# Bringing a softmax's reciprocals to a row: diagonal matrices on TensorE, or a trip through scratch memory

## The chip, the cores and the metric

The kernel runs on one core of a Trainium2 chip. The core has five engines that run side by side and meet at semaphores: TensorE (PE, matrix products into PSUM; its weight loads are shown apart as PEld), VectorE (DVE), ScalarE (ACT), GpSimd (POOL), and SyncE (SP), which here only issues DMAs. Each engine has a queue of its own, in the order in which the program holds its instructions. The metric is the device time of one execution in microseconds (us); lower is better.

## The reference

One layer of an encoder with four token mixers side by side (a long convolution "hyena", a state space "S5", differential attention and latent attention), an output projection, a gated feed-forward net and an embedding gate, for 2048 tokens of width 1024. What matters here are the two attentions, each with 4 heads and values of width 64:

```
# differential attention, per head
attn = softmax(s1) - lam * softmax(s2)      # s1, s2: scores with an ALiBi bias
o    = attn @ v
# latent attention, per head
a    = softmax(s);  o = a @ v
```

Every softmax divides a row of exponentials, a query's, by its sum.

## The kernel before, in words

The kernel is written against a scheduler: the program lists work in an order with priorities, and the scheduler sorts each engine's instructions by its own estimate of when each can start. Two kinds of work are interleaved in the stage that matters. One is attention; the other is a background queue of the other mixers (filters, S5, embedding, the hyena convolution, output weights), advanced a little after every step of attention.

`Attention.run` (line 394) walks 64 units: 4 heads times 16 blocks of 128 queries. A unit handles one head of each attention at once, since both share the stage's shape. Its steps are 12 calls of `chunk`, and beside each the pieces of the unit one or two before it, by a table `PLAN`:

- `chunk` and `scores` (lines 421 and 438): TensorE makes scores of 128 queries by 512 keys in a PSUM bank (line 448), VectorE moves them to SBUF and takes minima (lines 451, 453), and when a row of 2048 is whole, ScalarE exponentiates it in place and sums it (line 458). The sum of a query lies on that query's partition, as `total`, 128 x 1.
- `combine` (line 460) joins the two score rows of the differential attention, on VectorE and, for some heads, GpSimd (lines 465 to 475).
- `scale(hd)` (line 477), once for each of the two attentions: VectorE takes the reciprocal of the sums (line 481), GpSimd multiplies the identity by it, which gives a 128 x 128 diagonal matrix `diag` (line 483).
- `transpose` (line 486): TensorE turns the exponentials so that keys lie on partitions (line 492), ScalarE copies them out of PSUM (line 497).
- `weigh(piece)` (line 499), 8 pieces, two units late: TensorE multiplies the values with them into a PSUM tile `ps_o`, whose partitions are the 64 channels of one head and the 64 of the other, and whose columns are the 128 queries (line 509, shown as L502 in the profile, where the helper is). The result has the queries along a row, whereas the reciprocals lie down a column. So after the last piece, a 128 x 64 matrix of ones is multiplied with each `diag` (line 519, again L502), which puts the 128 reciprocals in a row on all 64 partitions of that head, in the second half of the same PSUM tile. ScalarE copies that row to SBUF (line 523), VectorE multiplies (line 524), and every second unit ScalarE's queue issues two DMAs that write the result to `mixT` in scratch memory (line 527).

`ps_o` has one buffer. Query tiles `q_sb` have two, so a unit's five query loads (lines 381 to 383), on SyncE's queue, wait until the unit two before has made its last scores. The same queue carries the background's loads and stores: in the stretch of the hyena convolution these are `h_f`, `h_g` and `h_sp` (lines 1233 to 1237), each with two buffers. At a head's end it carries ten loads of the next head's keys `k_sb` (lines 369 to 372), which wait for the last scores that read the old ones.

Of the kernel before, what the change touches and what calls it, by code (L numbers as in the profile page):

```python
# [11 lines left out]
F32 = mybir.dt.float32  # L12
# [3 lines left out]
AF = mybir.ActivationFunctionType  # L16
ALU = mybir.AluOpType
PSUM = bass.MemoryType.PSUM

SEQ = 2048  # L20
DM = 1024
# [319 lines left out]
class Attention:  # L341
# [6 lines left out]
    def __init__(self, ops, const, S, ctx):  # L348
        self.ops, self.tc, self.nc, self.S, self.ident = ops, ops.tc, ops.nc, S, const["ident"]
        self.strip, self.neg_lam = const["strip"], const["neg_lam"]  # L350
        pool = lambda name, bufs, **k: ctx.enter_context(ops.tc.tile_pool(name=name, bufs=bufs, **k))
        self.qp, self.kp, self.sp, self.atp = pool("at_q", 2), pool("at_k", 1), pool("at_s", 1), pool("at_t", AT_BUFS[0])
        self.sm, self.op, self.dp, self.vp = pool("at_sm", 4), pool("at_o", 2), pool("at_d", 4), pool("at_v", 1)
        self.ps_s = pool("at_pss", PSS[0], space=PSUM)
        self.ps_t = pool("at_pst", PSS[1], space=PSUM)
        self.ps_o = pool("at_pso", 1, space=PSUM)
        self.ones = self.vp.tile([128, 64], F32, name="at_ones")
        self.nc.vector.memset(self.ones, 1.0)
        self.k, self.v, self.evac = [None] * 4, [None] * 2, 0

    def keys(self, i, h):
# [51 lines left out]
class Unit:  # L413
# [63 lines left out]
    def scale(self, hd):  # L477

        at, nc = self.at, self.nc
        r = at.sm.tile([128, 1], F32, name="r1")  # L480
        nc.vector.reciprocal(r, self.total["s" if hd else "s1"])
        d = at.dp.tile([128, 128], F32, name="diag")
        nc.gpsimd.tensor_scalar(d, at.ident, r, 0.0, ALU.mult, ALU.add)
        self.scales[hd] = d

    def transpose(self, hd, g):
        at, nc = self.at, self.nc
# [11 lines left out]
    def weigh(self, piece):  # L499
# [2 lines left out]
        mm = lambda out, lhsT, rhs, first, last: nc.tensor.matmul(  # L502
            out, lhsT=lhsT, rhs=rhs, start=first, stop=last, skip_group_check=True)
        if piece == 0:
            self.ps = at.ps_o.tile([128, 2, 128], F32, name="ps_o")
        ps = self.ps
        for c in (2 * piece, 2 * piece + 1):
            for hd in range(2):
                inst = mm(ps[ts(hd, 64), 0], at.v[c // 8][:, c % 8, ts(hd, 64)], self.tiles[hd, c // 4][:, c % 4], c == 0,
                          c == 15)  # L510
                if c == hd == 0:

                    for k in range(2):
                        at.ops.after(inst, self.turned[k, 3])
        if piece % 4 == 3 and self.t == 15:
            at.values(piece // 4, self.h + 1)
        if piece == 7:
            for hd in range(2):
                mm(ps[ts(hd, 64), 1], at.ones, self.scales[hd], False, True)
            if self.t % 2 == 0:  # L520
                at.out = at.op.tile([128, 2, 128], F32, name="o_sb")
            o = at.out[:, self.t % 2]
            nc.scalar.activation(o, ps[:, 1], AF.Copy)
            nc.vector.tensor_mul(o, ps[:, 0], o)
            if self.t % 2:
                for hd in range(2):
                    nc.scalar.dma_start(at.S["mixT"][ds(256 * hd + 64 * self.h, 64), ds(128 * self.t - 128, 256)],
# [158 lines left out]
NH = 22  # L686
# [1027 lines left out]
def tile_hybrid_encoder(ctx, tc, A, out):  # L1714
# [2 lines left out]
    pool = lambda c, name, bufs, **k: c.enter_context(tc.tile_pool(name=name, bufs=bufs, **k))  # L1717
    S = {}
    for name, shape in (("zhyT", [768, SEQ]), ("zs5", [SEQ, 256]), ("c", [SEQ, 352]), ("vda", [SEQ, 256]),
                        ("vml", [SEQ, 256]), ("yhs", [SEQ, 512]), ("mixT", [512, SEQ]), ("h", [SEQ, DM]), ("fT", [8, 128, SEQ]), ("f2T", [8, 128, SEQ]), ("g", [NH, 128, SEQ]), ("emb", [SEQ, DM]),  # L1720
                        ("h2", [SEQ, DM]), ("hspec", [2, 2, 2, 16, 128, 128]), ("hyc", [6, 32, 128, 64]), ("hyq", [2, 64, 128, 64]), ("s5_win", [128, 16, 2, 2, 128]),
                        ("s5_wout", [128, 2, 16, 256]), ("s5_g", [16, 16, 496]), ("s5_m", [128, 2, 16, 256]), ("s5_a16", [128, 2, 2, 16])):
        S[name] = tc.dram_tile(shape, F32, name="d_" + name)
# [165 lines left out]
```

## Time and profile before

| | before |
|---|---|
| times of three runs | 3736.25, 3740.24, 3745.21 us |
| median | 3740.24 us |
| profiled execution: time / span in the trace | 3744.99 / 3743.2 us |
[...]
| TensorE, VectorE, ScalarE, GpSimd busy | 91%, 66%, 47%, 41% |
| units of attention | from 585 us to 1905 us of the span |

The profile is one execution. Busy time is the union of an engine's instructions; a wait is an idle stretch of an engine, put down to the instruction elsewhere that ended it. A DMA's issue stands on the queue that issued it, and its landing is counted from there. In the timeline, instructions of one line that follow each other are merged into one row with a count.

### The profile page before, as it was taken

What the parts mean: (1) busy time and instruction counts of PE and PEld (TensorE: products, weight loads), DVE (VectorE), ACT (ScalarE), POOL (GpSimd) and SP (SyncE); (2) the same over time, 40 slices, a digit from 0 to 9 for tenths busy, and PEclk for the clock granted to TensorE, in tenths of its full rate; (3) what the DMA queues carried; (4) which work ended last, traced back from release to release, by engine and by line L of the source; (5) the groups of instructions that cost most, each with busy time, mean ns of one, the idle gap of its engine ahead of it and who ended that gap; (6) DMA issues with size and microseconds to landing.
All of it is one profiled execution on the core that took longest, in us unless ns stands there. A gap on an engine that the chain in (4) does not pass through costs nothing. (4 is left out here: it accounts for less than half of the span.)

```text
span 3743.2 us, 56824 instructions
## 1 busy us (share of the span) xinstructions
PE 3423.1 (91%) x20582; PEld 2802.2 (75%) x20582; DVE 2455.0 (66%) x5109; ACT 1754.3 (47%) x2889; POOL 1553.0 (41%) x1423
## 2 busy tenths in 40 slices
PE   8999997887999899989999899999999987989787
PEld 6889875676778778767777678887888865867666
DVE  6667548974746455677667764447545578688877
ACT  5334316665667545577754443334333433333443
POOL 1324001681852022253355554445544544344554
PEclk9999997998999999999999899999999999999899
DMA  4544655327232795961054532223222254546554
GB/s 143 185 142 153 219 164 141 104 76 208 76 100 87 190 251 146 222 195 40 18 178 144 177 113 79 90 79 107 90 79 90 74 188 149 203 141 191 186 170 151
DMA packets 426698, 518.46 MB, mean 139 GB/s; under 512 B 117003, under 2 KB 319631, under 8 KB 422415
## 3 DMA queue, kind: packets, MB, share of 16 engines
q1 hardware_dynamic: 352368, 407.05, 36.8%
q10 hardware_dynamic: 74048, 107.76, 8.2%
q8 instruction: 163, 2.67, 0.3%
q14 instruction: 119, 0.97, 0.1%
HBM read 340.89 MB, written 178.01 MB: 139 GB/s over the span
## 5 line engine op out<-in xcount | busy, mean ns | idle before, releaser
L448 PE MATMUL ps_s<-k_sb,q_sb 96*128 96x512 f32 x1280 | 437.5, 444 | 53.8 <-DVE at_s L451 22.2
L823 PE MATMUL ps_st<-t_hi,s_hi 128*128 128x512 f32 x984 | 397.2, 404 | 51.8 <-DVE st_sum L850 21.2
L458 ACT ACTIVATE at_s<-at_s,least_s 128x2048 f32<-128x2048 f32 x192 | 384.2, 2003 | 88.3 <-DVE least_s L457 71.6
L453 DVE CUSTOM_DVE_ANT_0 at_s<-ps_s,strip 128x512 f32<-128x512 f32 x512 | 338.1, 685 | 111.2 <-PE ps_s L448 96.9
L823 PE MATMUL ps_st<-t_lo,s_hi 128*128 128x512 f32 x984 | 392.6, 399 | 10.3 <-DVE t_lo L41 10.2
L823 PE MATMUL ps_st<-t_hi,s_lo 128*128 128x512 f32 x984 | 391.7, 398 | 5.6 <-DVE s_lo L41 5.5
L40 ACT ACTIVATE s_hi<-s_raw 128x512 fp32r<-128x512 f32 (+1 forms) x336 | 206.8, 618 | 352.9 <-PE ps_st L823 290.4
L497 ACT ACTIVATE at<-ps_at 128x512 f32<-128x512 f32 x512 | 287.7, 595 | 164.0 <-PE ps_at L492 151.1
L472 POOL TENSOR_SCALAR at_s<-at_s,f 128x1024 f32<-128x1024 f32 (+1 forms) x48 | 89.9, 1872 | 659.9 <-DVE f L466 474.6
L41 DVE TENSOR_TENSOR s_lo<-s_raw,s_hi 128x512 fp32r<-128x512 f32 (+1 forms) x336 | 270.0, 806 | 137.7 <-ACT s_hi L40 137.5
L492 PE MATMUL ps_at<-ident,at_s 128*128 128x128 f32 x2048 | 318.4, 286 | 41.7 <-ACT at L497 31.8
L40 ACT ACTIVATE a_hi<-a_raw 128x512 fp32r<-128x512 f32 (+1 forms) x252 | 155.4, 618 | 403.2 <-PE ps_st L823 217.5
L492 PEld LDWEIGHTS ps_at<-ident,at_s 128*128 128x128 f32 x2048 | 250.9, 146 | 108.5 <-ACT at L497 43.4
L448 PEld LDWEIGHTS ps_s<-k_sb,q_sb 96*128 96x128 f32 x1280 | 230.6, 197 | 122.4 <-DVE at_s L451 37.4
L823 PE MATMUL ps_st<-b_hi,a_hi 128*128 128x512 f32 x656 | 263.8, 402 | 30.9 <-DVE st_row L912 12.3
L807 POOL TENSOR_TENSOR s_raw<-a_raw 128x512 f32<-128x512 f32 (+1 forms) x84 | 110.8, 1319 | 433.6 <-DMA a_raw<-d_g 148.7
L41 DVE TENSOR_TENSOR a_lo<-a_raw,a_hi 128x512 fp32r<-128x512 f32 (+1 forms) x252 | 235.3, 936 | 72.1 <-ACT a_hi L40 71.1
L502 PE MATMUL ps_o<-at,v_sb 128*64 128x128 f32 x4096 | 274.2, 287 | 4.4 <-ACT at L497 3.3
L823 PEld LDWEIGHTS ps_st<-t_hi,s_hi 128*128 128x128 f32 x984 | 190.4, 194 | 104.4 <-DVE st_sum L850 25.0
L502 PEld LDWEIGHTS ps_o<-at,v_sb 128*64 128x64 f32 x4096 | 239.5, 144 | 36.2 <-issue 23.3
L823 PE MATMUL ps_st<-b_lo,a_hi 128*128 128x512 f32 x656 | 261.3, 398 | 4.4 <-DVE b_lo L41 4.3
L823 PE MATMUL ps_st<-b_hi,a_lo 128*128 128x512 f32 x656 | 260.7, 397 | 0.0
(480 smaller groups left out, 8305.7 us busy)
## 6 DMA issues: line engine op xcount, KB each, us to landing
d_h<-st_row ACTq DMA_DIRECT2D x64, 512.0 KB, 3.2
st_row<-d_h SPq DMA_DIRECT2D x64, 512.0 KB, 4.3
a_raw<-in_w_gate_dram SPq DMA_DIRECT2D x44, 512.0 KB, 4.0
a_raw<-in_w_up_dram SPq DMA_DIRECT2D x44, 512.0 KB, 3.9
d_g<-st_row ACTq DMA_DIRECT2D x44, 512.0 KB, 2.9
f_mat<-in_c_dft_f_dram SPq DMA_DIRECT2D x32, 512.0 KB, 4.4
h_g<-in_c_hy_g_dram SPq DMA_DIRECT2D x32, 512.0 KB, 7.1
h_sp<-d_hspec SPq DMA_DIRECT2D x64, 256.0 KB, 6.9
```

Source lines behind the costliest of these rows:

```text
L40: nc.scalar.activation(hi, src, AF.Copy)
L41: nc.vector.tensor_sub(lo, src, hi.bitcast(F32))
L448: nc.tensor.matmul(ps, lhsT=lhs, rhs=rhs[:, ts(c, 512)], start=n == 0, stop=n == len(products) - 1)
L453: nc.vector.tensor_tensor_reduce(dst, ps, at.strip[:, ds(1920 - 128 * self.t + 512 * c, 512)], self.slope, 3e38, ALU.add, ALU.min, least)
L458: nc.scalar.activation(s, s, AF.Exp, bias=least, scale=-1.0, accum_out=self.total[name])
L472: nc.gpsimd.tensor_scalar(s2[:, n:], s2[:, n:], f, 0.0, ALU.mult, ALU.add)
L492: self.turned[hd, g] = nc.tensor.transpose(ps[:, j], src[:, ts(4 * g + j, 128)], at.ident)
L497: nc.scalar.activation(tile, ps, AF.Copy)
L502: mm = lambda out, lhsT, rhs, first, last: nc.tensor.matmul(out, lhsT=lhsT, rhs=rhs, start=first, stop=last, skip_group_check=True)
L807: eng.tensor_add(s1, a21, a22)
L823: nc.tensor.matmul(bank, lhsT=l[x][:, c], rhs=r[y], start=first and c + k == 0, stop=c == kb - 1 and k == 2, skip_group_check=True)
```

## The change

`scale` no longer makes a diagonal. After the reciprocal, SyncE's queue writes the 128 x 1 column to a row of a new scratch tensor `sums` in device memory (128 x 128, one row for each unit and attention), and reads that row back, repeated for the 64 partitions of the head, into one half of a new tile `scale` (128 x 128, four buffers, one for each unit). `weigh` makes no products with ones; `ps_o` is half as wide; ScalarE's copy goes; VectorE multiplies `ps_o` by `scale` directly. The matrix of ones and its memset go.

```
 def scale(self, hd):
     r = at.sm.tile([128, 1], F32, name="r1")
     nc.vector.reciprocal(r, self.total["s" if hd else "s1"])
-    d = at.dp.tile([128, 128], F32, name="diag")
-    nc.gpsimd.tensor_scalar(d, at.ident, r, 0.0, ALU.mult, ALU.add)
-    self.scales[hd] = d
+    if not self.scales:
+        self.scales[0] = self.scales[1] = at.dp.tile([128, 128], F32, name="scale")
+    row = at.S["sums"][2 * (16 * self.h + self.t) + hd]
+    nc.sync.dma_start(row.rearrange("(q o) -> q o", o=1), r)
+    nc.sync.dma_start(self.scales[hd][ts(hd, 64)], row[None, :].to_broadcast([64, 128]))
...
 def weigh(self, piece):
-        self.ps = at.ps_o.tile([128, 2, 128], F32, name="ps_o")
+        self.ps = at.ps_o.tile([128, 128], F32, name="ps_o")
...
     if piece == 7:
-        for hd in range(2):
-            mm(ps[ts(hd, 64), 1], at.ones, self.scales[hd], False, True)
...
-        nc.scalar.activation(o, ps[:, 1], AF.Copy)
-        nc.vector.tensor_mul(o, ps[:, 0], o)
+        nc.vector.tensor_mul(o, ps, self.scales[0])
```

The scheduler sorts the whole attention stage anew. Up to the first unit's end every engine's order is as before, and from the feed-forward net on it is nearly so. In the changed program line numbers are up to three lower. Three places follow.

TensorE, near the stage's end, around the products of unit 56 (`ps_o<-at,v_sb` are the products with the values, `ps_s` scores, `ps_at` transposes). Before:

```order
L492 MATMUL ps_at<-ident,at_s_18642 128x128 x4
L448 MATMUL ps_s<-k_sb,q_sb 128x512
L492 MATMUL ps_at<-ident,at_s_18642 128x128 x4
L502 MATMUL ps_o<-at,v_sb 64x128 x32
L502 MATMUL ps_o<-diag,at_ones 64x128 x2
L492 MATMUL ps_at<-ident,at_s 128x128 x5
L448 MATMUL ps_s<-k_sb,q_sb 128x512
```

In the changed program:

```order
L492 MATMUL ps_at<-ident,at_s_18534 128x128 x4
L502 MATMUL ps_o<-at,v_sb 64x128 x16
L446 MATMUL ps_s<-k_sb,q_sb 128x512
L502 MATMUL ps_o<-at,v_sb 64x128 x8
L492 MATMUL ps_at<-ident,at_s 128x128 x4
L446 MATMUL ps_s<-k_sb,q_sb 128x512
L502 MATMUL ps_o<-at,v_sb 64x128 x8
L492 MATMUL ps_at<-ident,at_s 128x128 x4
```

The two products with ones are gone, and this unit's 32 products with values stand in three pieces between other work instead of in a row.

SyncE's queue in the last 200 us of the stage, one unit (before, the five query loads are all that stands there; `d_sums` is the scratch tensor, `r` the reciprocals). Before:

```order
L381 DMA q_sb<-d_qda 32x2x128 x3
L382 DMA q_sb<-d_qmn 64x2x128
L383 DMA q_sb<-d_qmr 32x2x128
```

In the changed program:

```order
L379 DMA q_sb<-d_qda 32x2x128 x3
L380 DMA q_sb<-d_qmn 64x2x128
L381 DMA q_sb<-d_qmr 32x2x128
L483 DMA d_sums<-r_17880 128x1
L483 DMA d_sums<-r_17893 128x1
L484 DMA scale<-d_sums 64x128 x2
```

Two writes and two reads stand between one unit's query loads and the next one's; each read waits for its write.

SyncE's queue in the hyena convolution, where the filters' loads of several steps stand around a unit's row. Before:

```order
L1253 DMA d_hyq<-h_q 128x512 x2
L1233 DMA h_f<-in_c_hy_f_dram 128x512 x2
L1237 DMA h_sp<-d_hspec 64x2x512 x4
L1234 DMA h_g<-in_c_hy_g_dram 128x1024
L1253 DMA d_hyq<-h_q 128x512
```

In the changed program:

```order
L483 DMA d_sums<-r_15685 128x1
L1250 DMA d_hyq<-h_q 128x512
L483 DMA d_sums<-r_15710 128x1
L484 DMA scale<-d_sums 64x128
L1231 DMA h_g<-in_c_hy_g_dram 128x1024
L1250 DMA d_hyq<-h_q 128x512
L484 DMA scale<-d_sums 64x128
L1230 DMA h_f<-in_c_hy_f_dram 128x512 x2
L1234 DMA h_sp<-d_hspec 64x2x512 x4
```

The next step's filter loads stand behind both reads of the unit's rows.

## Rows read from the trace of the kernel before

**Rows 1.** The page: busy us, share of the span, instructions; slices in tenths.

```profile
PE 3423.1 (91%) x20582; PEld 2802.2 (75%) x20582; DVE 2455.0 (66%) x5109; ACT 1754.3 (47%) x2889; POOL 1553.0 (41%) x1423
...
PE   8999997887999899989999899999999987989787
```

**Rows 2.** Busy by stretch: window, length, engines (instructions), clock, DMA share, GB/s.

```profile
585.00:1905.00 1320.00, 1173.03 (x9980) 960.87 (x9979) 860.37 (x2421) 834.16 (x1209) 535.93 (x577) 0.94 0.47 131
...
1280.00:1640.00 360.00, 331.58 (x2923) 277.07 (x2924) 210.85 (x583) 195.78 (x288) 91.23 (x71) 0.97 0.84 214
...
1700.00:1900.00 200.00, 182.81 (x1662) 149.35 (x1662) 131.93 (x436) 145.31 (x215) 71.23 (x61) 0.97 0.10 30
```

**Rows 3.** TensorE's waits, 585 to 1905: total us, times, longest us.

```profile
PE ps_at L492 <- ACT at L497: 31.8, 33, 2.4
PE ps_s L448 <- DVE at_s L451: 21.5, 29, 3.2
...
PE ps_hy L1214 <- DMA h_g<-in_c_hy_g_dram: 9.2, 7, 2.2
```

**Rows 4.** Busy by stretch, as rows 2, one of 20 us.

```profile
1330.00:1350.00 20.00, 20.00 (x155) 18.58 (x157) 9.34 (x25) 9.70 (x14) 1.21 (x1) 0.86 1.01 273
```

**Rows 5.** Groups by line, TensorE, 585 to 1905: count | busy us, mean ns.

```profile
L502 PE MATMUL ps_o<-diag,at_ones 128*64 128x128 f32 x256 | 29.4, 277 | 0.0
```

**Rows 6.** Timeline, TensorE: start, us, what, count, idle before.

```profile
851.52 3.71 PE L502 MATMUL ps_o<-at,v_sb 128*64 128x128 f32 x64
855.07 0.39 PE L502 MATMUL ps_o<-diag,at_ones 128*64 128x128 f32 x4
855.38 0.50 PE L448 MATMUL ps_s<-k_sb,q_sb 96*128 96x512 f32 x1
```

**Rows 7.** Instructions of tiles o_sb and diag: count, ns min/median/max.

```profile
L523 ACT ACTIVATE o_sb<-ps_o x64: 254/277/300, 605.1 to 1898.8; 128x128 f32<-128x128 f32 x64
...
L483 POOL TENSOR_SCALAR diag<-ident,r x128: 362/372/2393, 585.8 to 1889.2; 128x128 f32<-128x128 f32 x128
```

**Rows 8.** All waits, 585 to 1905, as rows 3.

```profile
DVE o_sb L524 <- ACT o_sb L523: 88.4, 31, 7.3
...
ACT o_sb L523 <- PE ps_o L502: 82.9, 40, 6.2
```

**Rows 9.** The waits of SyncE's own queue, 585 to 1905.

```profile
SPq L381 <- PE ps_s L448: 305.6, 44, 18.5
```

**Rows 10.** Timeline, all engines, the end of one unit.

```profile
1743.92 0.29 DVE L524 TENSOR_TENSOR o_sb<-ps_o,o_sb 128x128 f32<-128x128 f32 x1 [4.31 <-ACT o_sb L523]
...
1744.51 0.69 DVE L453 CUSTOM_DVE_ANT_0 at_s<-ps_s,strip 128x512 f32<-128x512 f32 x1 [0.29 <-PE ps_s L448]
```

**Rows 11.** The load of a 128 x 1 column (line 230): issue, landing.

```profile
L230 SPq DMA_DIRECT2D gq<-in_mla_g_q_dram x1: 352/352/352, 395.3 to 395.3; - x1
...
DMA to landing us min/median/max: 2.1/2.1/2.1
```

**Rows 12.** The results' writes (line 527), 1200 to 1660 us.

```profile
L527 ACTq DMA_DIRECT2D d_mixT<-o_sb x18: 452/466/663, 1240.0 to 1621.9; - x18
...
DMA to landing us min/median/max: 2.2/6.0/7.7
```

**Rows 13.** The same line, 1660 to 1905 us.

```profile
DMA to landing us min/median/max: 2.0/2.2/5.2
```

**Rows 14.** The query loads (line 381), 1200 to 1660 us.

```profile
DMA to landing us min/median/max: 1.7/2.9/9.5
```

**Rows 15.** Timeline, VectorE: reciprocals (line 481) and multiplies (line 524).

```profile
857.46 0.21 DVE L481 RECIPROCAL r<-total_s 128x1 f32<-128x1 f32 x2
...
866.23 0.29 DVE L524 TENSOR_TENSOR o_sb<-ps_o,o_sb 128x128 f32<-128x128 f32 x1 [6.58 <-ACT o_sb L523]
...
1724.89 0.22 DVE L481 RECIPROCAL r<-total_s 128x1 f32<-128x1 f32 x2
...
1885.74 0.22 DVE L481 RECIPROCAL r<-total_s 128x1 f32<-128x1 f32 x2 [0.31 <-ACT at_s L458]
...
1899.16 0.29 DVE L524 TENSOR_TENSOR o_sb<-ps_o,o_sb 128x128 f32<-128x128 f32 x1 [4.83 <-ACT o_sb L523]
```

More of the change, by code (lines that the diff above doesn't have):

```diff
@@ L356, in __init__ @@
         self.ps_o = pool("at_pso", 1, space=PSUM)
-        self.ones = self.vp.tile([128, 64], F32, name="at_ones")
-        self.nc.vector.memset(self.ones, 1.0)
         self.k, self.v, self.evac = [None] * 4, [None] * 2, 0
@@ L508, in weigh @@
             for hd in range(2):
-                inst = mm(ps[ts(hd, 64), 0], at.v[c // 8][:, c % 8, ts(hd, 64)], self.tiles[hd, c // 4][:, c % 4], c == 0,
+                inst = mm(ps[ts(hd, 64)], at.v[c // 8][:, c % 8, ts(hd, 64)], self.tiles[hd, c // 4][:, c % 4], c == 0,
                           c == 15)
@@ L1719, in tile_hybrid_encoder @@
     for name, shape in (("zhyT", [768, SEQ]), ("zs5", [SEQ, 256]), ("c", [SEQ, 352]), ("vda", [SEQ, 256]),
-                        ("vml", [SEQ, 256]), ("yhs", [SEQ, 512]), ("mixT", [512, SEQ]), ("h", [SEQ, DM]), ("fT", [8, 128, SEQ]), ("f2T", [8, 128, SEQ]), ("g", [NH, 128, SEQ]), ("emb", [SEQ, DM]),
+                        ("vml", [SEQ, 256]), ("yhs", [SEQ, 512]), ("mixT", [512, SEQ]), ("sums", [128, 128]), ("h", [SEQ, DM]), ("fT", [8, 128, SEQ]), ("f2T", [8, 128, SEQ]), ("g", [NH, 128, SEQ]), ("emb", [SEQ, DM]),
                         ("h2", [SEQ, DM]), ("hspec", [2, 2, 2, 16, 128, 128]), ("hyc", [6, 32, 128, 64]), ("hyq", [2, 64, 128, 64]), ("s5_win", [128, 16, 2, 2, 128]),
```

## The prediction

> **What bounds the kernel now.** I read the page's engine shares and slices first, then the busy times by stretch, then who waits for whom inside the stretch that the change touches, and last the timelines at the places where its work sits. The page [rows 1] shows TensorE busy 91% of the span and nearly level over all 40 slices; no other engine is over 66%. The change acts in the attention stage alone, 585 to 1905 us, 64 units (a head's block of 128 queries) of 20.6 us on average. There [rows 2] TensorE is busy 1173.0 of 1320 us, VectorE 860.4, ScalarE 834.2, GpSimd 535.9: 147 us of TensorE are idle, and the reader is to see that this is little. What ends those gaps [rows 3]: ScalarE's copies of transposed blocks (31.8 us), VectorE's evacuation of scores (21.5), and the hyena filters' loads (9.2). So a matmul taken away is worth about its own slot, and a step off TensorE is worth something only where it sits in front of one of those copies.
>
> From 1280 to 1640 us a second resource is near its limit: the DMA share is 0.84 there [rows 2], and a stretch of 20 us inside has 1.01 [rows 4]. TensorE is at 92% in the same window, so both are tight together. In the last 200 us of the stage the DMA share is 0.10 [rows 2].
>
> **The change part by part.**
>
> *Products with ones.* 128 matmul calls go; the trace holds each as two instructions, 256 in all, 29.4 us as a union that overlaps its neighbours [rows 5]. The slot is read from the queue's pace: 64 products of `weigh` from 851.52 to the first product with ones at 855.07 are 55 ns each, and the next work starts 0.31 us after that first one [rows 6]. Between 4 x 55 = 0.22 and 0.31 us for a unit, 64 units give 14 to 20 us. I take 15, nearer the pace, since the change of tile that the upper end holds will still have to be paid behind the last real product.
>
> *ScalarE's copy of the row.* 64 copies of 277 ns go, 17.7 us [rows 7]. They are worth more as a wait: ScalarE stood idle 82.9 us in front of them until TensorE was done, VectorE 88.4 us in front of the multiply until the copy was done [rows 8]. Both engines work their queues in order, so what stands behind waited too: the copies of transposed blocks, the scores. But the timeline of one handover [rows 10] shows how little reaches TensorE: the multiply ends at 1744.21, and the next thing that VectorE does still waits 0.29 us for TensorE. So from 0 up to all 31.8 us that TensorE waited for ScalarE's copies; I take a quarter, 8 us, being nearer the handover shown.
>
> *Diagonals.* 128 GpSimd instructions of 372 ns go, 48 us [rows 7]. GpSimd is 41% busy in the stage [rows 2] and none of TensorE's larger gaps names a diagonal [rows 3], so 0. The ones and their memset are nothing.
>
> *The way through scratch.* Four more DMAs per unit on SyncE's queue: two writes of 128 x 1, two reads of a 512-byte row into 64 partitions. Neither shape is in the trace. The nearest to the write is the load of a column of 128 x 1: 352 ns to issue, 2.1 us to land [rows 11]; the 64 KB write of the head's result lands in a median 6.0 us from 1200 to 1660 us, at most 7.7 [rows 12], and in 2.2 after that [rows 13]. The read is like the query loads: 1.7 us at least, median 2.9, at most 9.5 in the loaded stretch [rows 14]. So from reciprocal to row 4 us where it is quiet, 9 us in the loaded stretch, 17 at worst. Below nothing is excluded, since a transfer gives nothing back. Does that reach the end? The multiply comes well after the reciprocal: 1724.89 to 1743.92 is 19.0 us, 1885.74 to 1899.16 is 13.4 for the last unit, and 857.46 to 866.23 is 8.8, the shortest of all 64 [rows 10, 15]. So the row is there in time nearly always; the cover is the work of one whole unit, and where it is gone VectorE stands, and the scores behind the multiply with it.
>
> *SyncE's queue.* The reads wait for the writes' landing, and SyncE issues in order. The order of the changed program puts write, write, read, read between one unit's query loads and the next; behind them are the hyena and embedding loads. In the tail this is free: the queue holds nothing else, and SyncE already stands 305.6 us of the stage until TensorE frees the query buffers [rows 9]. In 1280 to 1640 SyncE is held 6 us (the landing) once per unit while double-buffered filter loads stand behind it. The DMA engines still have what was issued before; they run dry only for about one landing of a quiet transfer, 2 us, and TensorE sees that only where it was about to wait anyway. Of the 18 units that issue [rows 12] some 15 end in that window: from 0 to 15 x 4 = 60 us (two quiet landings of 2 us in each, with nothing queued), and I take 5, nearer the 9.2 us that the filter loads cost now [rows 3]. At two of the three head changes the reads of an earlier unit (14, 30) now stand behind ten key loads, which wait for the old head's last scores; but the new head's scores wait for the same keys, so this is a read's landing at most, 2 to 3 us each, inside the 5.
>
> *Order.* The scheduler re-sorts the stage. In the tail the before had whole bursts of 32 products, the after splits most of them between scores and transposes. No duration says what that is worth: the handover just behind a burst, at 1743 us, has VectorE waiting for TensorE and not the reverse [rows 10]. I take 0, and 10 us either way in the range.
>
> **The sum.** -15 - 8 + 5 = -18 us. Against the profiled execution's 3745.0 us that gives 3727. That run is 4.8 us over the median of the runs shown, 3740.2; from the median it is 3722, the number I give.
>
> [...] TensorE's starts in [rows 6] follow each other without a gap, and matmul busy is 89% of the stage. [...]
>
> [...] Rows show a landing of 2.2 us when quiet and 6.0 when loaded. [...]
>
> **The rivals.**
> A, the forecast, 3722: -8 to -33 us. For it: the gaps of TensorE are short and its queue is paced. Chance 0.50.
> B, no difference, 3740 (within 7.5 us, about what a measurement here can tell, 0.2%): the products fill slots, or the gain in the quiet parts is given back in the loaded ones. For it: the ScalarE and VectorE waits removed end where TensorE's own work ends. Against: [rows 6]. Chance 0.20.
> C, slower, 3757: SyncE held at the writes in the loaded stretch. Place: 1280 to 1640 us and the head changes near 1290 and 1630, where key loads stand in the same queue. Price: two thirds of the upper end, 2.7 us per unit over 15 units, is 40 us, less 23 gained = +17; it ends slower once the hold costs over 23 / 15 = 1.5 us per unit. For it: DMA share 0.84 to 1.01, 6 us landings, loads only two deep, a queue in order. Against: TensorE lost only 9.2 us to those loads so far. Chance 0.26.
> D, the row comes after the products in most units, so that VectorE and ScalarE stand at the multiply as before, now for a DMA: it would take landings near 8 us each way in all units; 64 x 1 us less 15 = 3790. The 13 to 19 us of cover speak against it. Chance 0.04.
>
> **How the numbers follow.** The likeliest is A: 3722, its own range 3705 to 3732. For 8 in 10 the range must take B and the lower half of C: 3702 (pace at its upper end, 20, and half of the ScalarE waits) to 3762. Faster by over 0.2%: 0.51; within: 0.21; slower: 0.28, from the same cases.
>
> **What would show it.** Right: TensorE has 256 fewer instructions, VectorE's wait before the multiply names TensorE and not a DMA, TensorE is busy some 15 us less in the stage than 1173, and TensorE's idle time from 1280 to 1640 us is as before, 28.4 us (360 less 331.6). Wrong: multiplies that name the scale row's DMA; more TensorE waits on filter loads than 9.2 us, or new ones on keys and values; landings of the 128 x 1 writes far over 6 us; or a stage elsewhere that the new order made worse by more than the 10 us allowed.

## The result, and the profile after

The changed kernel takes 3993.39 us (median of four runs, 3985.25 to 4001.28) against 3741.28 us for the kernel before on the same chip: a ratio of 1.067, 95% interval 1.066 to 1.069. That is 252 us slower where 18 us faster was forecast, and far outside the range of 3702 to 3762. The profiled execution of the changed kernel has a span of 3988.2 us.

The page of the changed kernel first: span, busy times with their share of the span, and three of the rows in 40 slices.

```profile
span 3988.2 us, 56466 instructions
...
PE 3475.4 (87%) x20326; PEld 2839.0 (71%) x20326; DVE 2469.2 (62%) x5108; ACT 1740.0 (44%) x2825; POOL 1512.2 (38%) x1295
...
PE   8999987787689687886899989999999998889887
...
PEclk9999998888799888897999989999999999999898
...
DMA packets 455369, 522.70 MB, mean 131 GB/s; under 512 B 137484, under 2 KB 348304, under 8 KB 451088
```

TensorE has its 256 instructions less (20582 in [rows 1]) and is nevertheless busy 52 us longer. In slices 6 to 20, which lie in the attention stage, its busy share is mostly 6 to 8 tenths where [rows 1] has 7 to 9, and the granted clock (PEclk) is at 7 or 8 tenths in ten of the fifteen. The DMA queues carried 28,700 packets more.

Now by stretch: window, length, busy us of TensorE, its weight loads, VectorE, ScalarE and GpSimd (instructions), granted clock, DMA share, GB/s. The last multiply of attention is at 2136.8 us; before it was at 1899.2.

```profile
585.00:2136.80 1551.80, 1218.80 (x9684) 989.19 (x9684) 863.11 (x2411) 817.35 (x1140) 477.47 (x443) 0.88 0.46 113
585.00:1900.00 1315.00, 1009.79 (x7869) 820.34 (x7869) 703.84 (x1914) 652.18 (x912) 400.05 (x397) 0.86 0.51 125
1900.00:2136.80 236.80, 209.00 (x1816) 168.85 (x1817) 159.26 (x498) 165.17 (x229) 77.42 (x46) 0.94 0.21 48
```

Beside [rows 2] (1173.0 busy of 1320 at a clock of 0.94) the stage has grown by 237.6 us to its last multiply; TensorE is idle 333 us in it instead of 147, which is 186 of the 237.6 us; the other 51 are busy time, for 256 instructions fewer at the lower clock. The rest of the difference between the two executions, 7 us, lies behind attention. Over the whole stage the DMA engines were no busier (share 0.46, before 0.47) and moved less in the same time (113 GB/s, before 131).

Who waits, in the attention stage (engine, line, what for: us in total, times, longest). SyncE's own queue, then VectorE at the multiply, then TensorE:

```profile
SPq L484 <- DMA d_sums<-r: 379.8, 76, 10.0
SPq L483 <- DVE r L479: 90.3, 26, 13.5
...
SPq L379 <- PE ps_s L446: 40.7, 20, 8.5
```

```profile
  PE ps_o L502: 89.2, 44
  DMA scale<-d_sums: 33.1, 4
```

```profile
PE ps_at L492 <- ACT at L497: 73.7, 32, 15.9
PE ps_s L446 <- DVE at_s L449: 28.5, 28, 10.9
PE ps_hy L1211 <- DMA h_g<-in_c_hy_g_dram: 28.4, 10, 8.3
PE ps_s L446 <- DVE four_s L451: 26.9, 11, 11.6
PE ps_hy L1465 <- POOL s_v L1296: 21.3, 3, 7.6
PE ps_s L446 <- DMA q_sb<-d_qda: 13.6, 1, 13.6
```

Lines 483 and 484 are the write of the column and the read of the row. SyncE, which stood 305.6 us for the query buffers [rows 9], now stands 379.8 us for its own writes to land. The multiply itself waits for the row in only 4 of 64 units: the cover that the prediction counted is there. TensorE's losses do not point to one place: the three lines of [rows 3] grew from 62.5 to 130.6 us, and loads that had hardly been waited for (filters, queries) and a step of GpSimd's stand beside them.

The pace of the units tells more. Mean distance of two multiplies, head by head, worked out from the 64 multiplies of each trace:

| head | before | after |
|---|---|---|
| 0 | 17.4 us | 22.7 us |
| 1 | 23.7 | 28.7 |
| 2 | 22.4 | 29.3 |
| 3 | 14.2 | 14.9 |
| 3, units 54 to 61 | 14.5 | 13.4 |

In the last head, when little other work loads anything [rows 2], the changed kernel loses least (0.7 us a unit against 5 to 7 in the others), and in the steady part of it, units 54 to 61, it is faster. And this although the way through scratch is slow there too. SyncE's queue around one of those units (start us, us to issue, what, count): the two writes go out at 2024.49, the reads can only follow 7.2 us later.

```profile
2024.49 0.81 SPq L483 DMA_DIRECT2D d_sums<-r  x2
2031.69 1.09 SPq L484 DMA_DIRECT2D scale<-d_sums  x2
```

So the landing is long everywhere (6.8 us or more from write to read in each of the 64 units), but seems to cost only where other transfers are under way. The experiments start from there.

### The profile page after: what moved, and what is told of

The parts are those of the page before. It is cut to its first block, busy times and chain, and to the rows that moved or that the text cites. A ratio compares the mean times of both kernels' runs of the same rounds, so it can differ in the third digit from the quotient of the medians.

```text
span 3988.2 us, 56466 instructions
## 1 busy us (share of the span) xinstructions
PE 3475.4 (87%) x20326; PEld 2839.0 (71%) x20326; DVE 2469.2 (62%) x5108; ACT 1740.0 (44%) x2825; POOL 1512.2 (38%) x1295
## 5 line engine op out<-in xcount | busy, mean ns | idle before, releaser
L446 PE MATMUL ps_s<-k_sb,q_sb 96*128 96x512 f32 x1280 | 450.0, 455 | 89.8 <-DVE at_s L449 29.0
L492 PE MATMUL ps_at<-ident,at_s 128*128 128x128 f32 x2048 | 338.4, 298 | 85.6 <-ACT at L497 73.7
L492 PEld LDWEIGHTS ps_at<-ident,at_s 128*128 128x128 f32 x2048 | 266.1, 153 | 156.2 <-ACT at L497 84.1
L446 PEld LDWEIGHTS ps_s<-k_sb,q_sb 96*128 96x128 f32 x1280 | 238.6, 203 | 163.7 <-DVE at_s L449 47.2
L502 PE MATMUL ps_o<-at,v_sb 128*64 128x128 f32 x4096 | 290.4, 295 | 5.1 <-ACT at L497 4.1
L502 PEld LDWEIGHTS ps_o<-at,v_sb 128*64 128x64 f32 x4096 | 250.9, 149 | 41.0 <-issue 27.6
```

Of the source, the lines that this page charges most:

```text
L446: nc.tensor.matmul(ps, lhsT=lhs, rhs=rhs[:, ts(c, 512)], start=n == 0, stop=n == len(products) - 1)
L492: self.turned[hd, g] = nc.tensor.transpose(ps[:, j], src[:, ts(4 * g + j, 128)], at.ident)
L502: mm = lambda out, lhsT, rhs, first, last: nc.tensor.matmul(out, lhsT=lhsT, rhs=rhs, start=first, stop=last, skip_group_check=True)
```

## The experiments

The expectations number the theories. T1 (and S) is SyncE's hold, the prediction's rival C: reads wait for landings, loads queue behind them. T2 is the new order of the stage. T3 is that the transfers of the trip hold up other transfers; it was later split into W (the writes of adjacent 4-byte values) and R (the reads of one row into 64 partitions). F1 names the write of a column into a row as the slow form of several. All ratios are to runs of the kernel before on the same chip, with 95% intervals.

**What a write of a column costs by itself.** `forms` does nothing but scratch transfers on SyncE, each write followed by a read that needs it, and writes zeros as its result.

```
...
row = D("row", [128, 128])                      # 128 values side by side
nc.sync.dma_start(row[5].rearrange("(q o) -> q o", o=1), src[:, 0:1])
nc.sync.dma_start(src[0:64], row[5][None, :].to_broadcast([64, 128]))
gap64 = D("gapb", [128, 16])                    # 64 bytes apart
nc.sync.dma_start(gap64[:, 0:1], src[:, 0:1])
nc.sync.dma_start(src[:, 0:1], gap64[:, 0:1])
...
```

> Only scratch writes and reads on SyncE's queue, each read waiting for its write, four rounds of eight forms; all of the reference's work is left out (the output is zeros). In the changed kernel a read is issued 7 to 9 us after its write even where nothing else uses the DMA engines. Theory F1 (128 values of 4 bytes next to each other in one 512-byte row of device memory are slow): the column to one row takes about 7 us until its read can issue, the same 128 values 64 or 512 bytes apart about 2 us, 64 or 512 bytes from every partition about 2 us, one row of 512 bytes from one partition about 2 us, 16 values about 2.5 us, two rows at once about 14 us. Theory F2 (128 separate pieces of 4 bytes are slow wherever they go): the column 64 or 512 bytes apart also takes 7 us, 64 bytes from every partition clearly less. Theory F3 (any write to device memory followed by a read of it takes 7 us): all eight take about 7 us.

Its SyncE queue, third round: d_row is the column of 128 values into 512 bytes, d_gapb the same values 64 bytes apart, d_one a whole row from one partition, d_two two columns into two rows, d_few 16 values side by side.

```profile
107.02 0.34 SPq L1721 DMA_DIRECT2D d_row<-src  x1
116.13 0.45 SPq L1722 DMA_DIRECT2D src<-d_row  x1
118.57 0.33 SPq L1724 DMA_DIRECT2D d_gapb<-src  x1
119.99 0.32 SPq L1725 DMA_DIRECT2D src<-d_gapb  x1
...
130.94 0.24 SPq L1736 DMA_DIRECT2D d_one<-src  x1
132.03 0.45 SPq L1737 DMA_DIRECT2D src<-d_one  x1
134.40 0.38 SPq L1739 DMA_DIRECT2D d_two<-src  x1
142.62 0.45 SPq L1740 DMA_DIRECT2D src<-d_two  x1
146.77 0.33 SPq L1742 DMA_DIRECT2D d_few<-src  x1
148.08 0.45 SPq L1743 DMA_DIRECT2D src<-d_few  x1
```

The column takes 9.1 us from issue to issue here, 7.6 to 9.1 over the four rounds, on a core that does little else. The same 128 values 64 bytes apart take 1.4 us, a row from one partition 1.1. It is not the number of values and not a fixed cost of any transfer; it is that they are neighbours. Two columns into two rows were expected at twice the time of one and took 8.2 us, as long as one, as if the two rows went side by side.

**The removals without the trip.** `no_trip` multiplies by a tile of ones and sends nothing to scratch, so its result is not divided by the sums.

```diff
...
-        row = at.S["sums"][2 * (16 * self.h + self.t) + hd]
-        nc.sync.dma_start(row.rearrange("(q o) -> q o", o=1), r)
-        nc.sync.dma_start(self.scales[hd][ts(hd, 64)], row[None, :].to_broadcast([64, 128]))
+        self.scales[0] = at.flat
```

> The changed kernel without the trip: no scratch writes and no reads; the multiply takes a constant tile of ones instead of the reciprocals, so the softmax's division is left out. Theory T1 (SyncE held at the writes' landing makes the time): the 253 us are gone and the removals show their worth; by the quiet tail of the changed kernel, 13.35 us a unit against 14.6 before, up to 64 x 1.2 = 80 us, so 3660 to 3725. Theory T2 (the removal of the products made the scheduler find a worse order): near 3990, at least over 3850. Theory T3 (the extra small packets load the DMA engines): as T1.

3758.66 us, 1.0044 (1.0029 to 1.0059). T2 falls: removals and new order together lose 16 us, not 250. The gain that T1 and T3 expected of the removals (3660 to 3725 us) did not come either, which the part on the prediction comes back to. What the trip adds is about 235 us.

**SyncE's hold taken away, twice.** `read_later` issues the reads only after the unit's last transposes; `pool_queue` issues writes and reads from GpSimd.

```diff
...
+        at.ops.after(inst, self.turned[0, 3])             # inst: the read
...
-        [(1, T, 0, 3)], [], []]
+        [(1, T, 0, 3), (1, F, 0), (1, F, 1)], [], []]     # F: the two reads
```

> The changed kernel, with each read placed behind the unit's last transposes, some 10 us after the write, so that other loads stand between them on SyncE's queue and the write has landed when the read comes up. All DMAs stay as they are. Theory T1: SyncE is held for little, 3670 to 3760. Theory T2 (a worse order from the removals): over 3850. Theory T3 (load on the DMA engines from the small packets): near 3990, since they are all still there.

> The changed kernel with both the writes and the reads issued by GpSimd instead of SyncE. Theory T1: SyncE is free again; GpSimd is held instead, and its own work (the joining of two score rows, S5's products) comes late by up to 7 us a unit: 3700 to 3850. T2: over 3850, since the order is about the same. T3: near 3990.

3979.38 us, 1.0623 (1.0591 to 1.0654), and 4014.02 us, 1.0721 (1.0694 to 1.0748). SyncE's waits in the first, and those of SyncE and of GpSimd in the second:

```profile
SPq L379 <- PE ps_s L446: 152.8, 34, 13.2
SPq L481 <- DVE r L479: 120.3, 33, 15.7
...
SPq L489 <- DMA d_sums<-r: 81.1, 16, 10.2
```

```profile
SPq L379 <- PE ps_s L446: 318.0, 45, 20.4
```

```profile
POOL scale L484 <- DMA d_sums<-r: 473.7, 77, 12.8
```

In `read_later` SyncE stands for landings 81 us instead of 380, in `pool_queue` not at all: it stands for query buffers as in the kernel before. The first gives back half a point of 6.7, the second none, and both stay near the 3990 us of T3. Moving the wait to GpSimd does not help: it then stands 473.7 us for the same landings. T1 is not the main cause.

**Writes or reads.** `write_only` is the kernel before, all its work included, plus the column writes, which nobody reads. `gap_only` is the same with the values 64 bytes apart. `read_only` has the reads and no writes.

```diff
...
         self.scales[hd] = d
+        row = at.S["sums"][2 * (16 * self.h + self.t) + hd]                       # write_only: these two lines
+        nc.sync.dma_start(row.rearrange("(q o) -> q o", o=1), r)
...
+        gap = at.S["sums"][2 * (16 * self.h + self.t) + hd].rearrange("(q o) -> q o", o=16)   # gap_only: these two
+        nc.sync.dma_start(gap[:, 0:1], r)
```

> The kernel before, computing all it did (diagonals, products with ones), plus the 128 writes of a column of reciprocals into one 512-byte row of scratch, which nothing reads. The changed kernel took 250 us more than before, the one without the trip 16 us more, so the trip as a whole is worth about 235 us. Theory W (the writes of 128 adjacent 4-byte values hold up other transfers): nearly all of it comes back although nobody waits for these writes, 3900 to 3990 us, and transfers' packets of over 2 us, of which the attention stage of before has none and that of the changed kernel 243, are there by the hundred. Theory R (the reads of one row into 64 partitions do it): 3735 to 3765 us and no such packets. Theory S (SyncE's hold): 3735 to 3765 us too, since SyncE waits for no write here.

> The same writes as in write_only, 128 of 128 values of 4 bytes, but each value 64 bytes from the next in scratch, and read by nobody; all else is the kernel before. Theory W, in the form that the adjacency is what costs (a column landed in 1.4 us with the values 64 bytes apart and in 7.6 us side by side): 3735 to 3765 us, no packets of over 2 us. If the mere number of 4-byte packets or of transfers does it: the time of write_only, 3900 us or more.

> The changed kernel without its writes: scratch is filled once with ones ahead of attention, and each unit reads its two rows into 64 partitions each and multiplies by them, so that the result is left undivided by the sums. Theory W: within 1% of the kernel without the trip, 3745 to 3790 us. Theory R: 3900 us or more.

| kernel | median us | ratio | interval |
|---|---|---|---|
| write_only | 3920.20 | 1.0465 | 1.0446 to 1.0484 |
| gap_only | 3766.84 | 1.0052 | 1.0033 to 1.0070 |
| read_only | 3796.62 | 1.0127 | 1.0100 to 1.0154 |

The first two decide it. They differ in where 128 values of 4 bytes go in scratch memory, by nothing else, and nothing reads what they write; one is 153 us slower than the other. Their traces hold the same instructions in the same order on every engine and every queue, so no new order can make the difference. `gap_only` lies just above the range expected of it, and so does `read_only`, some 30 us above the kernel without the trip by the ratios: the reads, or the queue that holds them, cost something, but not the 3900 us of theory R. Both by stretch, the same 1295 us, `write_only` first:

```profile
585.00:1880.00 1295.00, 1053.78 (x8337) 857.14 (x8337) 718.22 (x2013) 700.82 (x1006) 459.70 (x512) 0.88 0.58 129
```

```profile
585.00:1880.00 1295.00, 1137.67 (x9558) 927.07 (x9557) 835.34 (x2332) 801.12 (x1152) 511.38 (x551) 0.93 0.48 131
```

TensorE gets through 8337 instructions instead of 9558, at a clock of 0.88 against 0.93, while the DMA engines are busier (0.58 against 0.48) for the same GB/s. TensorE's waits in `write_only` are spread as in the changed kernel (ScalarE's copies 50.3 us, h_g 22.0).

The records of single packets say how. Packets that took more than 2 us, between 585 us and the last multiply of attention, counted from each trace:

| kernel | over 2 us | longest |
|---|---|---|
| before | 0 | 1.8 us |
| no_trip, gap_only, read_only | 1 each | 2.0 to 2.3 |
| keep_diag, runs, runs4, read_only4, runs_pair, runs_pair_pool (below) | 0 to 3 | 1.7 to 2.3 |
| write_half (below) | 354 | 7.2 |
| write_only | 488 | 8.3 |
| after | 243 | 7.4 |
| read_later | 421 | 8.3 |
| pool_queue | 492 | 8.9 |

The long ones are not the 4-byte packets (9 ns at the median by their records) but those of other transfers: in the changed kernel 215 of the 243 are of 1 to 16 KB and none is of 4 bytes.

**Spacing, number, and a load beside it.** `forms2` varies the spacing and then times a 512 KB load on ScalarE's queue alone, beside a column write from SyncE, and beside a spaced one.

```
nc.vector.memset(big[:, 0:1], 0.0)
nc.sync.dma_start(col, src[:, 0:1])             # or nothing, or 64 bytes apart
nc.scalar.dma_start(big, x[ds(512 * n + 128, 128)])
nc.vector.tensor_copy(seen, big[:, 0:1])        # shows the landing
```

> A kernel of scratch transfers alone; what the reference computes is left out and zeros are written. On SyncE each write is followed by a read that needs it, so the distance of the two issues is the landing. Theory W says that values in one 64-byte piece of memory are written one behind the other: 16 of them took 1.3 us, 128 values side by side 7.6 us, 128 values 64 bytes apart 1.4 us. If each piece is a queue of its own, 128 side by side would take as long as 16, so it must be more than the piece: expected are 7.6 us at 4 bytes, and with the values 8, 16 and 32 bytes apart still some 7 us as long as the row of neighbours is what counts, or 4, 2 and 1.4 us if the number in a piece counts; 32 and 64 side by side 2 and 4 us by a fixed time for each value. Sixteen bytes from each partition 7 us by value count, 4 runs of 128 bytes 1.1 to 1.4 us. After that a load of 512 KB on ScalarE's queue, alone, with the column's write issued just ahead on SyncE, and with the spaced write: alone 4 to 5 us; theory W: with the column 4 to 7 us more, with the spaced write under 1 us more. If the loss comes only of waits on the write itself, all three alike.

From write to read, in the three rounds after the first: 7.8 to 10.1 us with the values 4 bytes apart, 3.1 to 3.7 at 8 bytes, 1.4 to 2.4 at 16, 1.4 to 1.7 at 32; 32 values side by side 3.2 to 3.5, 64 side by side 7.0 to 7.3; 16 bytes from each of the 128 partitions, side by side, 1.4 to 2.0; four runs of 128 bytes 1.6. One count puts these in order: how many of the pieces lie in the same 256 bytes of memory. 64 of them cost 7 to 10 us (as 64 values in all, as 128 in 512 bytes, or as 256 in two rows in `forms`, 8.2 us), 32 cost 3.1 to 3.7, 16 cost 1.3 to 2.4 (the 16-byte pieces, expected at 7 us, among them). From 32 to 64 that is about 0.11 us a piece, an estimate from those rows. So it looks as if neighbours within 256 bytes went one behind the other, and different stretches of 256 bytes side by side; what in the memory does this, no run shows.

Now the load, third round, all engines (L1750 alone, L1756 beside the column d_qa, L1762 beside the spaced d_qb; the copies into seen start when the load has landed):

```profile
252.08 0.33 ACTq L1750 DMA_DIRECT2D big<-in_x_dram  x1
255.43 0.15 DVE L1751 COPY seen<-big 128x1 f32<-128x1 f32 x1 [3.38 <-DMA big<-in_x_dram]
...
255.80 0.32 SPq L1755 DMA_DIRECT2D d_qa<-src  x1
255.83 0.34 ACTq L1756 DMA_DIRECT2D big<-in_x_dram  x1
267.58 0.15 DVE L1757 COPY seen<-big 128x1 f32<-128x1 f32 x1 [11.80 <-DMA big<-in_x_dram]
...
267.95 0.32 SPq L1761 DMA_DIRECT2D d_qb<-src  x1
267.98 0.34 ACTq L1762 DMA_DIRECT2D big<-in_x_dram  x1
271.72 0.15 DVE L1763 COPY seen<-big 128x1 f32<-128x1 f32 x1 [3.78 <-DMA big<-in_x_dram]
```

A load of 512 KB on another engine's queue, to other memory, lands in 3.4 us alone, in 3.8 beside the spaced write and in 11.8 beside the column of 512 bytes (11.4 to 11.8 in the three rounds after the first): 8.4 us more than alone, about as long as the two one behind the other. What holds the load up in that time, the trace does not show.

**A write that is not slow.** `runs` and `runs4` turn the column on VectorE first, so that four partitions hold 32 values each, and write four runs of 128 bytes; the reads, and SyncE's wait for the landing, stay. The turning took VectorE about 0.2 us each time, not the 0.1 expected. The diff is that of `runs4`; `runs` has three buffers for the rows on all partitions instead of four, and two tiles for the columns to turn instead of one. `read_only` has three buffers as well; `read_only4` is the same with four.

```diff
-        r = at.sm.tile([128, 1], F32, name="r1")
-        nc.vector.reciprocal(r, self.total["s" if hd else "s1"])
+        nc.vector.reciprocal(at.column[:, 0:1], self.total["s" if hd else "s1"])
+        r = at.sm.tile([128, 32], F32, name="r1", bufs=2)
+        nc.vector.transpose(r, at.column)                   # blocks of 32 x 32
...
-        nc.sync.dma_start(row.rearrange("(q o) -> q o", o=1), r)
+        nc.sync.dma_start(row.rearrange("(k j) -> k j", j=32), r[0:128:32])
```

> The changed kernel with the column turned on VectorE first (32 by 32 blocks), so that scratch gets four runs of 128 bytes instead of 128 values of 4 bytes; the reads of one row into 64 partitions, the wait of SyncE for the write and the place of all steps stay as they are. 128 more instructions on VectorE of about 0.1 us. Theory W: 3740 to 3800 us, SyncE held for the write some 1 to 2 us at a time instead of 5 (379.8 us over 76 waits), no packets of over 2 us. Theory R: 3900 us or more, since the reads are all there.

> The kernel with the column turned on VectorE and four runs of 128 bytes written, now with four buffers for the rows on all partitions as in the changed kernel (the first of its kind had three, and its last units took 15.7 us each against 13.4). If the third buffer's lack cost the cadence: 3755 to 3775 us, last units 13.4 us. If not: 3783 us as before. Faster than the kernel before (under 3735 us) only if the removed products pay here as they didn't without the trip.

> The reads alone with four buffers; the writes are left out, and the result is not divided by the sums. If the reads themselves cost little and the third buffer's lack was the 38 us above the kernel without the trip: 3755 to 3775 us, last units 13.4 us. If the reads cost: 3790 us or more.

`runs`: 3782.95 us, 1.0098 (1.0078 to 1.0119). `runs4`: 3761.31 us, 1.0039 (1.0024 to 1.0054). `read_only4`: 3784.99 us, 1.0102 (1.0085 to 1.0118). With its whole trip, `runs4` is where the kernel without a trip is (1.0044): some 235 us of the changed kernel's loss are gone with the shape of the write. SyncE's waits in it, and then its longest in `read_only4`:

```profile
SPq L486 <- DVE r L482: 176.0, 45, 15.9
SPq L381 <- PE ps_s L448: 138.6, 45, 11.5
SPq L487 <- DMA d_sums<-r: 55.4, 58, 4.9
```

```profile
SPq L487 <- DVE o_sb L524: 194.0, 37, 15.8
```

In `runs4`, 58 waits for a landing are 1.0 us each instead of 5. What was expected of the fourth buffer's effect on the last units did not come: they run at 15.7 us with three buffers and with four, so that the time of `runs4` lies in its range for another reason than the one given, and which is open. And `read_only4`, which leaves more out than `runs4`, is slower than it; in it SyncE comes to the reads early and stands 194.0 us until the multiply gives the buffer free, with the loads of other work behind. I read it as a hold of the queue, but no run takes that hold away from it, so the price of the reads alone stays open between 0 and some 22 us (the difference of its ratio to that of the kernel without the trip).

**What keeps the repaired step from a gain.** `keep_diag` is the kernel before without the two products and ScalarE's copy, GpSimd's diagonals kept. `runs_pair` turns both heads' columns at once and needs one write and one read for a unit; `runs_pair_pool` issues these from GpSimd; both have three buffers for the rows, where `runs4` has four. `write_half` writes one head's column only.

```diff
-            for hd in range(2):
-                mm(ps[ts(hd, 64), 1], at.ones, self.scales[hd], False, True)     # keep_diag
...
-            nc.scalar.activation(o, ps[:, 1], AF.Copy)
-            nc.vector.tensor_mul(o, ps[:, 0], o)
+            nc.vector.tensor_mul(o, ps[:, 0], at.strip[:, 0:128])
```

```diff
...
+        nc.vector.transpose(r, at.column)                   # runs_pair: 128 x 64, both heads
...
+        nc.sync.dma_start(rows.rearrange("h (k j) -> k h j", j=32), r[0:128:32].rearrange("k (h j) -> k h j", h=2))
+        nc.sync.dma_start(self.scales[0], rows[:, None, :].to_broadcast([2, 64, 128]))
```

> The kernel before without the two products with ones and without ScalarE's copy of their result; GpSimd still makes the diagonals, nothing is sent to scratch, and the multiply takes constants, so that the result is not divided by the sums. If the removals are worth the 23 us of the prediction and the kernel without the trip only drew a bad order: 3715 to 3730 us. If the removals' gain is small or is given back in the order of the rest in any case: 3735 to 3765 us.

> Both heads' columns are turned on VectorE in one instruction, written with one transfer of eight runs of 128 bytes and read back with one transfer into 128 partitions: half the transfers of runs4. In the program's order of the last units TensorE's transposes, scores and products stand as in the changed kernel (13.4 us a unit) and not as in runs4 (15.7 us). If the order is what runs4 lost: about 20 to 36 us less than runs4's 3761 us, 3722 to 3745 us, last units 13.3 to 13.6 us. If SyncE's hold for the reciprocals and the landing is what it lost: 3750 to 3765 us, since SyncE still waits once for each unit.

> runs_pair with both transfers issued by GpSimd, so that SyncE holds no transfer behind a reciprocal or a landing. If SyncE's hold still costs in runs_pair: 10 to 20 us less than it. If not: within 8 us of it, or more, where GpSimd's part of the combination comes late behind the landing.

> The kernel before with the column's write for one of the two heads only, 64 writes instead of the 128 of write_only (4.65% over before), read by nobody. Theory W by the number of writes: half, 2.0 to 2.6%, 3820 to 3845 us. If the loss is a wait that any write of a unit sets: as write_only, 3900 us or more.

| kernel | median us | ratio | interval |
|---|---|---|---|
| keep_diag | 3752.59 | 1.0015 | 1.0004 to 1.0026 |
| runs_pair | 3799.13 | 1.0169 | 1.0154 to 1.0184 |
| runs_pair_pool | 3747.55 | 1.0033 | 1.0020 to 1.0047 |
| write_half | 3865.23 | 1.0351 | 1.0334 to 1.0368 |

`keep_diag` says that the removals are worth nothing at the end. `runs_pair` lies 34 us above the higher of its two ranges: the order of the last units, from which a gain was expected, was there in part (14.3 us a unit), and the whole was slower. Its SyncE stands in front of the write until the second head's sums are there; the waits of lines 489 and 490:

```profile
SPq L489 <- DVE least_s L457: 68.1, 12, 12.2
SPq L490 <- DMA d_sums<-r: 65.6, 51, 4.3
SPq L489 <- DVE r L485: 44.7, 18, 9.2
```

With the same two transfers issued by GpSimd the time falls by 52 us, where 10 to 20 were expected, and the last units run at 13.4 us. So SyncE's hold seems to have a price, of up to some 50 us here: the mechanism of rival C is likely real, only not the cause of the 250 us. The price is an upper bound, since the scheduler sorted the two kernels differently on nearly every engine, and no run takes the hold away with the order kept. `runs_pair_pool` is the best form of the step that was found, some 240 us better than the changed kernel by the ratios, and still 0.33% slower than the kernel before; no kernel here beats that one. `write_half` was expected at half the loss of `write_only` and shows three quarters (and 354 long packets to 488): the loss is no fixed price for each write. What fits is that the two writes of a unit leave within 1.5 us of each other in 59 of the 64 units of `write_only`, and that two columns into two rows took no longer than one in `forms`: leaving out one of the two leaves as many moments at which a write is under way. That it is this was not tried.

**Where the removals' gain goes.** In `no_trip` TensorE is busy 1149.91 us up to the last multiply, in the kernel before 1167.73, and attention ends 13.3 us earlier (1885.9 against 1899.2). In `keep_diag` it is 0.9 us earlier. The 13.3 us can be scatter between executions: the one of `no_trip` that was profiled is the fastest of ten, 10.8 us under their median, and that of the kernel before is 3.7 us over its own. Behind attention both lose: the products 329 to 656 of the 6888 into the tiles `ps_st` (the large matrix products behind attention, split by Strassen's method), which the change does not touch, take 114 to 117 us in all eleven kernels without the products with ones and 102 to 105 us in the four kernels with them. These stretches in the kernel before and in `no_trip`:

```profile
2009.00:2112.00 103.00, 99.36 (x523) 80.61 (x523) 77.50 (x205) 43.21 (x90) 60.88 (x79) 0.98 0.49 154
```

```profile
1994.00:2109.00 115.00, 105.31 (x535) 85.06 (x534) 83.04 (x213) 42.14 (x88) 64.99 (x77) 0.93 0.42 135
```

The same products, some of the output projection between them, 6 us more of idle TensorE, and a clock of 0.93 where it was 0.98. Most of the added idle time is that in front of products whose operand `s_hi` ScalarE makes: 6.1 us in three waits, where the kernel before has 0.4 in one. That the scheduler put that stretch in another order fits it being the same in eleven kernels; it was not tried with the old order, so why ScalarE comes late there stays open.

## Why the prediction was wrong, point by point

**The way through scratch** is the step that failed, in two places. First its landing: priced from the load of a 128 x 1 column (2.1 us) and a write of 64 KB (2.2 to 6.0 us), 4 us in all where it is quiet. From the issue of a unit's first write to that of its first read it was 6.8 us at least, 7 to 10 in 48 of the 64 units and more in 15, and 7.6 to 9.1 us in `forms`, where little else runs. Neither of the two rows has what made it slow, many small pieces going into one place of memory: [rows 11] goes to 128 partitions, [rows 12, 13] write long runs. Second, and far dearer: the sum asked who waits for this write (SyncE, the multiply) and not what else it holds up. That term was not in the sum at all. Measured by `write_only` against `gap_only` it is 153 us, with nobody who reads the values. The trip costs some 235; the 80 us between the two come only where the values are waited for and read, they are gone too when the write is quick (`runs4`), and no run takes them apart further.

**The cover** was right: 4 of 64 multiplies wait for the row, and rival D, at 0.04, did not come.

**SyncE's queue**, +5 with an end of 60, and rival C at 40 gross: `gap_only`, whose SyncE stands 137.7 us for the reciprocals and for no landing, costs 19 us, and `runs_pair` costs 52 us more than `runs_pair_pool`, both with other changes of order in them. So the end of 60 holds as far as these runs go, and 5 was probably too low as the likeliest value. Rival C had the direction right and the cause wrong: its 3757 us are 236 short.

**Products with ones**, -15, and **ScalarE's copy**, -8: the products' slot may be there in `no_trip` (17.8 us less busy, 13.3 us earlier, as far as one fast execution tells), and in `keep_diag` it is not (0.5 us less). TensorE's waits for ScalarE's copies, of which a quarter was to go, were 31.8 us before, 52.4 without the trip and 31.0 in `keep_diag`. Nothing of the 23 us is left at the end of either kernel. The sentence that a matmul taken away is worth about its own slot was wrong as a statement on the end. Without the trip the time is near that of rival B: by the ratios 6 us over the kernel before in `keep_diag`, within B's 7.5, and 16 in `no_trip`, beyond it. What fits is B's second reason, a gain given back, though behind attention and not in its loaded part.

**Diagonals**, 0: no gain came of leaving them out. The kernel with them, `keep_diag`, is at 1.0015, the one without, `no_trip`, at 1.0044; the two are sorted differently.

**Order**, 0 with 10 us either way: too narrow. The last units run at 13.3 to 15.9 us in kernels with nearly the same steps in another order, and the stretch behind attention takes some 11 us more.

Of the signs named as "wrong", three came in full: landings of the writes over 6 us, TensorE's waits on filter loads (h_g 9.2 to 28.4 us), and a stretch elsewhere that is slower by more than 10 us, the one behind attention. Multiplies that name the row's DMA came in 4 units. "Right" came the 256 instructions and the multiply that names TensorE, and neither decided anything; TensorE's busy time went up and not down by 15 us. Two ends of ranges do not follow from their terms: 20 us and half of 31.8 below 3740 are 3704 and not 3702, and 33 below 3740 is 3707 and not 3705. Neither matters beside 252 us.

## What to carry to other kernels

Before a small transfer is added to a busy stage, ask two things of it: what waits for it, and what it makes wait. A column of 4-byte values from 128 partitions into one row of memory was the costly form here. Turned on the chip into runs of 128 bytes, the whole trip cost no more than leaving it out (235 us before), with every wait still in its place, only shorter; spacing the values took the unread write from 174 us to 19. And a wait that dominates an engine's list (SyncE's 379.8 us) is a suspect and not a proof: a kernel in which the work stays and nobody needs its result settles that.

## What the runs showed of the hardware

- Values of 4 bytes that went into the same 256 bytes of scratch memory landed as if written one behind the other, about 0.11 us each by an estimate from `forms2` (32 in 3.1 to 3.7 us, 64 in 7.0 to 7.3); 128 of them 64 bytes apart landed in 1.4 us (`forms`).
- While such a write was under way, other transfers took longer: a 512 KB load on another queue 11.4 to 11.8 us instead of 3.3 to 3.4 (`forms2`), and single packets of other transfers took up to 8.9 us (`pool_queue`) where before none was over 1.8.
- A small write and the read that needs it followed each other in 1.1 to 1.6 us on a quiet core (a row from one partition in `forms`, four runs of 128 bytes in `forms2`).
- In the attention stage the mean granted clock was 0.94 before, with TensorE idle for 147 us, and 0.88 after, with 333 us idle and 51 us more busy time to the last multiply for 256 instructions less. The clock's records hold two levels, full speed and half of it: half speed covers 160 us of the stage before and 383 us after. Which of the two, gaps or clock, came first is not shown.
